# Gate and up of a SwiGLU layer in rows: both in one matmul of 512 columns, their gated product transposed on TensorE

## The chip, the cores and the metric

The kernel runs on one core of one Trainium2 chip. The metric is the device time of one execution in microseconds (us). The time of the kernel before is the median of three runs. Beside them stands one execution taken by the hardware profiler, from which the profile and the trace come.

## The reference

A hybrid decoder layer over 256 tokens of width 1024, in float32: a mixer (causal pooling and block attention) with an output projection, a cross-attention into 256 memory tokens, and a SwiGLU layer of width 2816, each with a residual and a LayerNorm behind it. The change touches the last of these:

```python
def swiglu(h, w_gate, w_up, w_down):
    return (jax.nn.silu(h @ w_gate) * (h @ w_up)) @ w_down
...
        h = layer_norm(DEEPNORM_ALPHA * h + swiglu(h, w_gate[l], w_up[l], w_down[l]),
                       ln3_g[l], ln3_b[l])
```

## The kernel before

**Three products.** Every large matmul is formed from float32 operands split in two parts, a rounded part ("h") and the rest ("l"). `three` (L217 to L221) issues three matmuls into one accumulator: h x h (L219), h x l (L220), l x h (L221). `split` (L275 to L277) makes the two parts of an activation: a cast on ScalarE (ACT) and a subtraction on VectorE (DVE).

**The weights.** `Stream` holds every weight as a list of tiles in the order of use, each 128 partitions by 1024 float32 (512 KB). For a tile, `prepare` (L68) issues the load on SyncE's queue (SP, L65, 4 raw buffers), casts it on ACT (L79) and subtracts on DVE (L80; 8 buffers for the result). `get` prepares at most one more tile at each call, up to six ahead of those that are used up (`AHEAD`), unless `held` is set; `done` counts a tile as used. The order of all instructions is the order in which the program emits them: nothing is reordered on an engine, so a cast, a Silu and a split stand in one queue on ACT, and a subtraction and a product in one on DVE. PSUM has two pools of four banks: `accbank` and `bank`.

**Before the layer.** The norm of token block 1 (128 of 256 tokens) ends while gate and up of chunk 0 are already formed for token block 0. `transpose_tok` (L283 to L289) turns the normed rows `h2` into `h2T` (channels on partitions): four transposes on TensorE (PE) into one bank (`tp`, L287), then a split.

**Gate and up.** The width of 2816 is done in 11 chunks of 256. For chunks 1 to 10 (L730 to L741) `proj_t` (L228) makes the product transposed: a 128x128 block of the weight is the stationary operand, `h2T` with its 256 tokens the moving one; for each of two halves of the chunk it walks k = 0 to 7 (8 blocks of the width 1024), first for gate (`pg`), then for up (`pu`): 2 x 2 x 8 x 3 = 96 matmuls of 256 columns. Then one Silu on ACT (L738), one product on DVE (L739), each 128x512, and one split into `gT`. Chunk 0 alone is made in rows (`first_gu`, L703): a token block of `h2T` is stationary, 256 columns of the weight move, once for gate and once for up, for token block 0 and then for token block 1. Its gated rows `sg` are transposed on PE two at a time (`first_gu_t`, L712) into `pgt`: once inside token block 1 of chunk 0, once between gate and up of chunk 1.

**Down.** `project` (L564) forms the down projection from `gT` with a token block of `gT` stationary and 512 or 256 columns of the weight moving, in five pieces of the output; four of its accumulators are `accbank` banks, the fifth is a `bank`. Behind each piece follow parts of the last norm.

Of the kernel before, what the change touches and what calls it, by code (L numbers as in the profile page):

```python
# [8 lines left out]
F32 = mybir.dt.float32  # L9
F32R = mybir.dt.float32r  # L10
AF = mybir.ActivationFunctionType
# [3 lines left out]
P = 128  # L15
D = 1024
S = 256
T = S // P
KD = D // P
CW = 256  # L20
# [4 lines left out]
NFC = DFF // CW  # L25
# [8 lines left out]
PR_BUFS = 6  # L34
# [3 lines left out]
def r32(t):  # L38
    return t.bitcast(F32)
# [63 lines left out]
@with_exitstack  # L103
def decoder_layer(
    ctx: ExitStack, tc: tile.TileContext, x, x_t, mem_t, w_in, w_u, w_pool, pool_scale, w_out,
    ln1_g, ln1_b, w_xq, w_xk, w_xkv, w_xo, ln2_g, ln2_b, w_gate, w_up, w_down, ln3_g, ln3_b, out,
):
    nc = tc.nc
    cp = ctx.enter_context(tc.tile_pool(name="const", bufs=1))
# [2 lines left out]
    sp = ctx.enter_context(tc.tile_pool(name="small", bufs=3))  # L112
# [4 lines left out]
    def a8(name, dt=F32):  # L117
        return ap.tile([P, KD, S], dt, tag="a8", name=name)

    def bank(name):  # L120
        return pb.tile([P, 512], F32, tag="b", name=name)

    def accbank(name):
        return pa.tile([P, 512], F32, tag="acc", name=name)


    ws = Stream(nc, wp)

    def cols(w, c):

        return ws.add(w[c])

    def rows(w, k0, c0, nk=2, width=D):
        return ws.add(w[k0 * P:(k0 + nk) * P, c0:c0 + width].rearrange("(k p) n -> p k n", p=P))
# [7 lines left out]
    c_xv = [rows(w_xkv, k, D) for k in range(0, KD, 2)]  # L142
    c_xq = [cols(w_xq, c) for c in range(4)]
    c_xo = [rows(w_xo, k, 0) for k in range(0, KD, 2)]
    c_gu = [(cols(w_gate, c), cols(w_up, c)) for c in range(NFC)]
    c_dn = [rows(w_down, k, 0) for k in range(0, FB, 2)]


# [34 lines left out]
    def load_gb(i, g, b):  # L183
# [15 lines left out]
    ident = cp.tile([P, P], F32, name="ident")  # L199
# [4 lines left out]
        out=tri[:, P:], in_=tri[:, P:], compare_op=OP.is_ge, fill=NEG, base=0,  # L204
# [12 lines left out]
    def three(ps, w, y, start, stop):  # L217
        (wa, wb), (ya, yb) = w, y
        nc.tensor.matmul(ps, wa, ya, start=start, stop=False)  # L219
        nc.tensor.matmul(ps, wa, yb, start=False, stop=False)  # L220
        nc.tensor.matmul(ps, wb, ya, start=False, stop=stop)  # L221

    def pair(hl, *ix):
        return hl[0][ix], hl[1][ix]

    ALL = slice(None)

    def proj_t(pss, numbers, yT, last=True):  # L228

        for f in range(2):  # L230
            for k in range(KD):
                hi, lo = ws.get(numbers, k)
                s = slice(f * P, (f + 1) * P)
                three(pss[f], (hi[:, s], lo[:, s]), pair(yT, ALL, k), k == 0, k == KD - 1)
                if f == 1 and last:
                    ws.done(numbers, k)
                yield

    def proj_n(ps, numbers, yT, t, last=True):

        for k in range(KD):
            three(ps, pair(yT, ALL, k, slice(t * P, (t + 1) * P)), ws.get(numbers, k), k == 0, k == KD - 1)
            if last:
                ws.done(numbers, k)
            yield

    def proj_rows(acc, chunks, get, pieces, first, last, free):

        last_k = sum(ws.rows(numbers) for numbers in chunks) - 1
        k0 = 0  # L250
        for numbers in chunks:
            nk = ws.rows(numbers)
            for t in sorted({piece[0] for piece in pieces}):
                for j in range(nk):
                    k = k0 + j
                    y = pair(get(k), ALL, slice(t * P, (t + 1) * P))
                    hi, lo = ws.get(numbers, j)
                    for piece in pieces:
                        if piece[0] == t:
                            s = slice(*piece[1:])  # L260
                            three(acc[piece], y, (hi[:, s], lo[:, s]), first and k == 0, last and k == last_k)
                    if free and t == pieces[-1][0]:
                        ws.done(numbers, j)
                    yield
            k0 += nk

    def run(gen, n=None):

        while n is None or n > 0:
            if next(gen, gen) is gen:  # L270
                return False
            n = None if n is None else n - 1
        return True

    def split(h, l, ps):  # L275
        nc.scalar.copy(h, ps)  # L276
        nc.vector.tensor_sub(l, ps, r32(h))  # L277
# [234 lines left out]
    class Norm:  # L512
# [11 lines left out]
        def sum(self, c0, c1, acc):  # L524
            s = slice(c0, c1)
            nc.vector.scalar_tensor_tensor(self.r[:, s], self.tok[:, s], ALPHA, acc, op0=OP.mult, op1=OP.add)  # L526
# [37 lines left out]
    def project(chunks, get, held, pieces=PIECES):  # L564

        acc = {}
        for piece in pieces:
            acc[piece] = (accbank if len(acc) < 4 else bank)("acc")[:, :piece[2] - piece[1]]
        head, rest = chunks[:-held], chunks[-held:]
        done = sum(ws.rows(numbers) for numbers in head)  # L570
        if head:
            yield from proj_rows(acc, head, get, pieces, True, False, True)
        ws.prepare(ws.used + AHEAD)
        ws.prepare(ws.used + W_BUFS, nc.gpsimd)
        ws.held = True
        for piece in pieces:
            yield from proj_rows(acc, rest, lambda k: get(done + k), [piece], not head, True, piece == pieces[-1])
            yield piece, acc[piece]

    def until(gen):  # L580

        for got in gen:
            if got is not None:
                return got
# [97 lines left out]
    h2T = (a8("h2Th", F32R), a8("h2Tl", F32R))  # L682
    gT = [(a8(f"gTh{i}", F32R), a8(f"gTl{i}", F32R)) for i in range(3)]
# [16 lines left out]
    run(xo)  # L700


    def first_gu(t):  # L703
        ps = accbank("pgn")
        for i, numbers in enumerate(c_gu[0]):
            yield from proj_n(ps[:, i * CW:(i + 1) * CW], numbers, h2T, t, t == T - 1)
        sg = sp.tile([P, 512], F32, tag="pr", name="sg", bufs=PR_BUFS)[:, :CW]
        nc.scalar.activation(sg, ps[:, :CW], AF.Silu, bias=0.0, scale=1.0)
        nc.vector.tensor_mul(sg, sg, ps[:, CW:])
        yield sg  # L710

    def first_gu_t(t, sg):  # L712
        pt = bank("pgt")
        for f in range(2):
            nc.tensor.transpose(pt[:, f * P:(f + 1) * P], sg[:, f * P:(f + 1) * P], ident)
        ts = slice(t * P, (t + 1) * P)
        split(gT[0][0][:, 0:2, ts], gT[0][1][:, 0:2, ts], pt[:, :CW].rearrange("p (f t) -> p f t", f=2))

    gu0 = first_gu(0)
    run(gu0, 14)  # L720
    transpose_tok(h2T, h2[:, 1, :], 1, 0)
    run(gu0, 2)
    gu1 = first_gu(1)
    transpose_tok(h2T, h2[:, 1, :], 1, 4)
    sg0 = until(gu0)
    ws.held = False
    run(gu1, 6)
    first_gu_t(0, sg0)
    sg1 = until(gu1)
    for c in range(1, NFC):  # L730
        pg = accbank("pg").rearrange("p (f t) -> p f t", f=2)
        pu = bank("pu").rearrange("p (f t) -> p f t", f=2)
        run(proj_t([pg[:, f, :] for f in range(2)], c_gu[c][0], h2T))
        if c == 1:
            first_gu_t(1, sg1)
        run(proj_t([pu[:, f, :] for f in range(2)], c_gu[c][1], h2T))
        sg = sp.tile([P, 2, S], F32, name="sgt", tag="pr", bufs=PR_BUFS)
        nc.scalar.activation(sg, pg, AF.Silu, bias=0.0, scale=1.0)  # L738
        nc.vector.tensor_mul(sg, sg, pu)  # L739
        i, f = divmod(2 * c, KD)  # L740
        split(gT[i][0][:, f:f + 2, :], gT[i][1][:, f:f + 2, :], sg)  # L741


    def store(t, y, c0, c1):
# [1 line left out]

    pieces = PIECES[:3] + ((1, 512, 768), (1, 768, D))
    dn = project(c_dn, lambda k: (gT[k // KD][0][:, k % KD], gT[k // KD][1][:, k % KD]), 3, pieces)
    for t in range(T):
        norm = Norm(3, h2[:, t, :])  # L750
        for _, c0, c1 in [piece for piece in pieces if piece[0] == t]:
            acc = until(dn)[1]
            for c in range(0, c1 - c0, 256):
                norm.add(c0 + c, c0 + c + 256, acc[:, c:c + 256])
        norm.stats()
        aside = (D - 384, D)
        norm.centre(*aside)
        norm.centre(0, 512)
        norm.scale_aside(*aside)
        norm.scale(0, 512)  # L760
        store(t, norm.r, 0, 512)
        norm.centre(512, aside[0])
        norm.scale(512, aside[0])
        store(t, norm.r, 512, D)
# [1 line left out]


_INS = ["x", "x_t", "mem_t", "w_in", "w_u", "w_pool", "pool_scale", "w_out", "ln1_g", "ln1_b", "w_xq", "w_xk",
        "w_xkv", "w_xo", "ln2_g", "ln2_b", "w_gate", "w_up", "w_down", "ln3_g", "ln3_b"]


# [30 lines left out]
```

## Time and profile before

| what | value |
|---|---|
| median of 3 runs | 394.28 us (394.07 to 394.31) |
| the profiled execution's own time | 393.67 us |
| its span, first to last instruction | 391.6 us |
| instructions | 6504 |
| granted clock of TensorE | 0.996 |
| HBM read, over the span | 70.52 MB, 183 GB/s read and written |

How to read the profile: engines are PE (TensorE matmul), PEld (TensorE loading a stationary operand, which overlaps PE), DVE, ACT, POOL (GpSimd) and SP or SPq (the queue that issues loads). In a row of the timeline the first number is the start in us from the start of the span, the second the length in us; then engine, line of the kernel, operation, what it writes and reads, its shape, and in brackets idle time ahead of it with what ended that. Matmuls are pipelined and their ends are modelled, so one lists longer than the distance to the next; the distance from start to start is what a stream of them costs. In a row of a group, behind the bar stand busy us in total and mean ns of one, then idle us ahead of the group and what released it.

### The profile page before, as it was taken

The numbers are of one execution on the slowest core, as the hardware profiler recorded it, in microseconds if no ns is written. First come the engines' busy times: TensorE is split into PE (matmuls) and PEld (weight loads), VectorE is DVE, ScalarE is ACT, GpSimd is POOL, SyncE is SP. The second block draws the span as 40 slices with busy tenths as digits, with TensorE's granted clock in tenths as the row PEclk, the third lists the DMA queues.
The fourth block names the chain that finished last, engine by engine and source line by source line (L and its number), as shares of the span: only waits on it lengthen the run. The fifth ranks groups of instructions, "written<-read, shape, count | busy, mean of one in ns | idle before, by whom it ended". The sixth has DMA issues, their size and how long they took to land.

```text
span 391.6 us, 6504 instructions
## 1 busy us (share of the span) xinstructions
PE 381.3 (97%) x2651; PEld 353.6 (90%) x2651; DVE 244.6 (62%) x327; ACT 176.1 (45%) x253; POOL 31.0 (8%) x37
## 2 busy tenths in 40 slices
PE   8999999999999999999999999999999999999991
PEld 7997889898888899988899999999999998888881
DVE  2749998776388766656887744556644457543276
ACT  3745848455233645455245633355543335343000
POOL 1000006500420000001400000000000000000022
PEclk9999999999999999999999999999999999999998
DMA  7998544756606862234408756654445875753002
GB/s 239 336 329 273 200 166 148 273 174 228 236 9 220 281 251 109 110 107 161 162 3 279 241 177 216 216 179 173 144 170 197 277 258 163 256 175 108 1 27 82
DMA packets 21886, 71.99 MB, mean 184 GB/s; under 512 B 2784, under 2 KB 3552, under 8 KB 21728
## 3 DMA queue, kind: packets, MB, share of 16 engines
q1 hardware_dynamic: 21568, 71.05, 52.7%
q10 hardware_dynamic: 288, 0.52, 0.7%
q8 instruction: 21, 0.34, 0.3%
q14 instruction: 9, 0.07, 0.1%
HBM read 70.52 MB, written 1.05 MB: 183 GB/s over the span
## 4 chain that ended last, share of the span: by engine, by line
PE 95%; DMA 2%; DVE 1%; SPq 0%; ACT 0%; issue 0%; DVEq 0%
PE acc L220 9%; PE acc L219 9%; PE acc L221 9%; PE pu L219 6%; PE pu L220 6%; PE pu L221 6%; PE pqk L323 5%; PE pg L220 5%; PE pg L219 5%; PE pg L221 5%; PE pxk L219 2%; PE pxq L219 2%; PE pxq L221 2%; PE pxq L220 2%; PE pxk L220 2%; PE pxk L221 2%
## 5 line engine op out<-in xcount | busy, mean ns | idle before, releaser
L739 DVE TENSOR_TENSOR sgt<-sgt,pu 128x512 f32<-128x512 f32 x10 | 6.9, 688 | 42.4 <-PE pu L221 42.4
L276 ACT CAST gTh<-sgt 128x512 fp32r<-128x512 f32 x10 | 6.2, 620 | 56.5 <-DVE sgt L739 56.5
L537 POOL TENSOR_TENSOR rs<-rs,mhalf 128x1 f32<-128x1 f32 x6 | 5.5, 912 | 199.0 <-DVE rs L536 199.0
L526 DVE SCALAR_TENSOR_TENSOR r<-h,acc 128x256 f32<-128x256 f32 (+1 forms) x12 | 6.0, 502 | 11.5 <-PE acc L221 11.5
L356 ACT ACTIVATE pr<-pr,mx 128x128 f32<-128x128 f32 (+1 forms) x16 | 7.2, 449 | 11.0 <-DVE mx L367 10.7
L547 ACT ACTIVATE r<-r,rs 128x384 f32<-128x384 f32 x2 | 1.2, 616 | 22.8 <-POOL rs L537 22.8
L277 DVE TENSOR_TENSOR gTl<-sgt,gTh 128x512 fp32r<-128x512 f32 x10 | 6.9, 693 | 6.9 <-ACT gTh L276 6.9
L541 DVE SCALAR_TENSOR_TENSOR r<-r,mv,g 128x512 f32<-128x512 f32 (+2 forms) x14 | 10.7, 776 | 0.0
L356 ACT ACTIVATE xpr<-xs,mx 128x256 f32<-128x256 f32 x8 | 3.7, 469 | 12.4 <-DVE mx L367 12.4
L529 DVE BATCH_NORM_STATS2 st<-r 128x6 f32<-128x512 f32 (+1 forms) x16 | 9.0, 561 | 0.5
L429 POOL TENSOR_TENSOR win<-upad 128x271 f32<-128x271 f32 x4 | 3.6, 888 | 59.9 <-DVE pr L363 59.9
L80 POOL TENSOR_TENSOR w59l<-w59r,w59h 128x1024 fp32r<-128x1024 f32 x1 | 2.4, 2442 | 69.9 <-ACT w59h L79 69.9
L276 ACT CAST h2Th<-tp 128x512 fp32r<-128x512 f32 x4 | 2.3, 587 | 12.3 <-PE tp L287 12.3
L738 ACT ACTIVATE sgt<-pg 128x512 f32<-128x512 f32 x10 | 6.0, 596 | 3.6 <-PE pg L221 3.6
L552 DVE SCALAR_TENSOR_TENSOR h<-r,rs,b 128x512 f32<-128x512 f32 x8 | 6.0, 752 | 1.9 <-POOL rs L537 1.8
L277 DVE TENSOR_TENSOR xTl<-xr,xTh 128x512 fp32r<-128x512 f32 (+1 forms) x5 | 2.9, 580 | 6.2 <-ACT xTh L276 6.2
L429 POOL TENSOR_TENSOR win<-win 128x269 f32<-128x269 f32 (+2 forms) x6 | 6.7, 1118 | 0.5
L526 DVE SCALAR_TENSOR_TENSOR r<-xt,acc 128x512 f32<-128x512 f32 x4 | 2.7, 682 | 6.2 <-PE acc L221 6.2
L361 DVE RECIPROCAL sm<-sm 128x2 f32<-128x2 f32 x12 | 2.0, 165 | 5.9 <-ACT xpr L356 4.5
L367 DVE TENSOR_REDUCE mx<-xs 128x2 f32<-128x512 f32 x4 | 2.8, 691 | 4.4 <-PE xs L221 4.4
L79 ACT CAST w41h<-w41r 128x1024 fp32r<-128x1024 f32 x1 | 1.1, 1051 | 9.5 <-PE tp L287 9.5
L287 PE MATMUL tp<-ident,h 128*128 128x128 f32 x32 | 4.8, 274 | 0.1
(1075 smaller groups left out, 1661.8 us busy)
## 6 DMA issues: line engine op xcount, KB each, us to landing
g<-in_ln_g SPq DMA_DIRECT2D x3, 512.0 KB, 6.3
b<-in_ln_b SPq DMA_DIRECT2D x3, 512.0 KB, 6.9
mr<-in_mem_t SPq DMA_DIRECT2D x1, 1024.0 KB, 7.9
xt<-in_x SPq DMA_DIRECT2D x1, 1024.0 KB, 9.0
out<-r SPq DMA_DIRECT2D x4, 256.0 KB, 2.0
xr<-in_x_t SPq DMA_DIRECT2D x3, 256.0 KB, 6.3
w2r<-in_w_in SPq DMA_DIRECT2D x1, 512.0 KB, 7.0
w3r<-in_w_in SPq DMA_DIRECT2D x1, 512.0 KB, 7.8
```

Source lines behind the costliest of these rows:

```text
L219: nc.tensor.matmul(ps, wa, ya, start=start, stop=False)
L220: nc.tensor.matmul(ps, wa, yb, start=False, stop=False)
L221: nc.tensor.matmul(ps, wb, ya, start=False, stop=stop)
L276: nc.scalar.copy(h, ps)
L277: nc.vector.tensor_sub(l, ps, r32(h))
L323: nc.tensor.matmul(qk[i][:, f, :], w, y, start=k == 0 and f == 0 and n == 0, stop=k == KD - 1 and n == 2, skip_group_check=True)
L356: nc.scalar.activation(dst[:, j, :], src[:, j, :], AF.Exp, bias=mx[:, j:j + 1], scale=1.0, accum_out=sm[:, j:j + 1])
L429: nc.gpsimd.tensor_add(nxt[:, 2 * n - 1:], cur[:, 2 * n - 1:], cur[:, n - 1:PADW + S - n])
L526: nc.vector.scalar_tensor_tensor(self.r[:, s], self.tok[:, s], ALPHA, acc, op0=OP.mult, op1=OP.add)
L529: nc.vector.bn_stats(self.st[:, self.n, :], self.r[:, c0:c1])
L541: nc.vector.scalar_tensor_tensor(self.r[:, s], self.r[:, s], self.mv[:, 0:1], gb[self.i][0][:, s], op0=OP.subtract, op1=OP.mult)
L739: nc.vector.tensor_mul(sg, sg, pu)
```

## The change

All 11 chunks are formed in rows. Host code puts gate's and up's 256 columns of a chunk side by side in one array (`w_gu`), so that a weight tile holds two k of 512 columns where it held four of 256. `proj_n` takes several accumulators: for each k it issues three matmuls of 512 columns for token block 0 and three for token block 1, each block with its own `accbank`. Chunk 0 runs token block 0 first (7 steps, a `transpose_tok`, the last step, the second `transpose_tok`), then token block 1. `gated` makes Silu and product of one token block (128x256 each). `gated_t` transposes the gated rows of a chunk, four transposes into one bank, and splits them into `gT`; for chunk c - 1 it is issued three k steps into chunk c, for the last chunk four steps into the down projection.

```diff
-    c_gu = [(cols(w_gate, c), cols(w_up, c)) for c in range(NFC)]
+    c_gu = [ws.add(w_gu[c], 4) for c in range(NFC)]
...
-    def proj_n(ps, numbers, yT, t, last=True):
+    def proj_n(pss, numbers, yT, last=True):
         for k in range(KD):
-            three(ps, pair(yT, ALL, k, slice(t * P, (t + 1) * P)), ws.get(numbers, k), k == 0, k == KD - 1)
+            for t, ps in pss.items():
+                three(ps, pair(yT, ALL, k, slice(t * P, (t + 1) * P)), ws.get(numbers, k), k == 0, k == KD - 1)
             if last:
                 ws.done(numbers, k)
             yield
...
+    def gated(c, t, ps):
+        sg = sgs[c][:, t, :]
         nc.scalar.activation(sg, ps[:, :CW], AF.Silu, bias=0.0, scale=1.0)
         nc.vector.tensor_mul(sg, sg, ps[:, CW:])
...
+    def gated_t(c):
+        pt = bank("pgt").rearrange("p (f t) -> p f t", f=2)
+        for t in range(T):
+            for f in range(2):
+                nc.tensor.transpose(pt[:, f, t * P:(t + 1) * P], sgs[c][:, t, f * P:(f + 1) * P], ident)
+        i, f = divmod(2 * c, KD)
+        split(gT[i][0][:, f:f + 2, :], gT[i][1][:, f:f + 2, :], pt)
+
+    sgs = [sp.tile([P, T, CW], F32, name="sg", tag="pr", bufs=PR_BUFS)]
+    first = [accbank("pg") for t in range(T)]
+    gu0 = proj_n({0: first[0]}, c_gu[0], h2T, False)
+    run(gu0, 7)
     transpose_tok(h2T, h2[:, 1, :], 1, 0)
+    run(gu0)
+    gated(0, 0, first[0])
     transpose_tok(h2T, h2[:, 1, :], 1, 4)
     ws.held = False
+    run(proj_n({1: first[1]}, c_gu[0], h2T))
+    gated(0, 1, first[1])
     for c in range(1, NFC):
+        sgs.append(sp.tile([P, T, CW], F32, name="sg", tag="pr", bufs=PR_BUFS))
+        pss = {t: accbank("pg") for t in range(T)}
+        gu = proj_n(pss, c_gu[c], h2T)
+        run(gu, 3)
+        gated_t(c - 1)
+        run(gu)
+        for t in range(T):
+            gated(c, t, pss[t])
...
     dn = project(c_dn, lambda k: (gT[k // KD][0][:, k % KD], gT[k // KD][1][:, k % KD]), 3, pieces)
+    run(dn, 4)
+    gated_t(NFC - 1)
...
+    given["w_gu"] = np.concatenate([chunks(given["w_gate"]), chunks(given["w_up"])], axis=3)
```

More of the change, by code (lines that the diff above doesn't have):

```diff
@@ L105, in decoder_layer @@
     ctx: ExitStack, tc: tile.TileContext, x, x_t, mem_t, w_in, w_u, w_pool, pool_scale, w_out,
-    ln1_g, ln1_b, w_xq, w_xk, w_xkv, w_xo, ln2_g, ln2_b, w_gate, w_up, w_down, ln3_g, ln3_b, out,
+    ln1_g, ln1_b, w_xq, w_xk, w_xkv, w_xo, ln2_g, ln2_b, w_gu, w_down, ln3_g, ln3_b, out,
 ):
@@ L700, in decoder_layer @@
     run(xo)
[L703 to L707, printed above, removed]
+    def gated(c, t, ps):
+        sg = sgs[c][:, t, :]
         nc.scalar.activation(sg, ps[:, :CW], AF.Silu, bias=0.0, scale=1.0)
         nc.vector.tensor_mul(sg, sg, ps[:, CW:])
[L710 to L717, printed above, removed]
@@ L719, in decoder_layer @@
-    gu0 = first_gu(0)
-    run(gu0, 14)
+    def gated_t(c):
[7 more added lines that the diff above has]
+    first = [accbank("pg") for t in range(T)]
@@ L721, in decoder_layer @@
+    gu0 = proj_n({0: first[0]}, c_gu[0], h2T, False)
+    run(gu0, 7)
     transpose_tok(h2T, h2[:, 1, :], 1, 0)
-    run(gu0, 2)
-    gu1 = first_gu(1)
+    run(gu0)
+    gated(0, 0, first[0])
     transpose_tok(h2T, h2[:, 1, :], 1, 4)
-    sg0 = until(gu0)
     ws.held = False
-    run(gu1, 6)
-    first_gu_t(0, sg0)
-    sg1 = until(gu1)
+    run(proj_n({1: first[1]}, c_gu[0], h2T))
+    gated(0, 1, first[1])
     for c in range(1, NFC):
[L731 to L741, printed above, removed]
+        sgs.append(sp.tile([P, T, CW], F32, name="sg", tag="pr", bufs=PR_BUFS))
[6 more added lines that the diff above has]
+            gated(c, t, pss[t])
@@ L768 @@
 _INS = ["x", "x_t", "mem_t", "w_in", "w_u", "w_pool", "pool_scale", "w_out", "ln1_g", "ln1_b", "w_xq", "w_xk",
-        "w_xkv", "w_xo", "ln2_g", "ln2_b", "w_gate", "w_up", "w_down", "ln3_g", "ln3_b"]
+        "w_xkv", "w_xo", "ln2_g", "ln2_b", "w_gu", "w_down", "ln3_g", "ln3_b"]
 def kernel(**inputs):
@@ L790 @@
     given["w_u"], given["w_xk"] = chunks(given["w_in"][:, :512]), chunks(given["w_xkv"][:, :D])
-    for name in ("w_xq", "w_gate", "w_up"):
-        given[name] = chunks(given[name])
+    given["w_xq"] = chunks(given["w_xq"])
+    given["w_gu"] = np.concatenate([chunks(given["w_gate"]), chunks(given["w_up"])], axis=3)
     for name in _INS:
```

## The prediction

> **What bounds the kernel now.** I read the page first: busy shares, granted clock, the chain that ended last. Times are microseconds (us).
>
> ```profile
> PE 381.3 (97%) x2651; PEld 353.6 (90%) x2651; DVE 244.6 (62%) x327; ACT 176.1 (45%) x253; POOL 31.0 (8%) x37
> ...
> PEclk9999999999999999999999999999999999999998
> ...
> PE 95%; DMA 2%; DVE 1%; SPq 0%; ACT 0%; issue 0%; DVEq 0%
> ```
>
> TensorE (PE) is busy 97% of the span, its clock is granted in full, and 95% of the chain is PE. A busy PE proves little, since its ends are modelled; so the second view is who waited for whom, for PE alone.
>
> ```profile
> PE busy L299 <- POOL ident masks.py:199: 1.4, 1, 1.4
> PE pqk L323 <- DVE w2l L80: 0.6, 1, 0.6
> PE pqk L323 <- ACT w0h L79: 0.3, 1, 0.3
> ```
>
> That is all: PE waits 2.3 us, at the start. From then on the time is the sum of PE's spacings, start to start. In the gate and up stage a spacing taken away is a saving, and one added is a loss, one for one. Third view: two stretches side by side, one of 512-column matmuls, one of the gate and up stage (256 columns). The columns are length, then busy time and count of PE, PEld, DVE, ACT and POOL, then granted clock, DMA share and GB/s.
>
> ```profile
> 91.00:111.00 20.00, 20.00 (x90) 16.57 (x89) 11.85 (x16) 7.90 (x9) 5.75 (x3) 1.00 0.55 190
> 207.50:322.00 114.50, 114.50 (x956) 114.50 (x956) 61.63 (x62) 52.04 (x62) 0.00 (x0) 1.00 0.61 209
> ```
>
> With 256 columns the loading of stationary operands (PEld) never rests; with 512 it rests a sixth of the time. DVE and ACT are about half idle in the stage.
>
> **The change part by part.** *Fewer, longer matmuls.* One chunk is now 96 matmuls of 256 columns (gate and up, 2 halves, 8 k, 3 products). After, it is 48 of 512 columns (8 k, 2 token blocks, 3 products), with the activations stationary and the weights moving. The down projection already runs that form. The timeline of PE gives both spacings.
>
> ```profile
> 311.08 0.28 PE L219 MATMUL pg<-h2Th,w97h 128*128 128x256 f32 x1
> ...
> 322.60 0.40 PE L219 MATMUL acc<-w101h,gTh 128*128 128x512 f32 x1
> ```
> ```profile
> 371.08 0.39 PE L219 MATMUL acc<-w117h,gTh 128*128 128x512 f32 x1
> ...
> 375.16 0.39 PE L219 MATMUL acc<-w117h,gTh 128*128 128x512 f32 x1
> ```
>
> Chunk 10 lies between the first two rows: 96 matmuls in 11.52 us, 0.1200 each. Between the last two lie 6 weight tiles of 3 products: 18 matmuls in 4.08 us, 0.2267 each. Two of the short cost 0.2400, one of the long 0.2267: each pair replaced saves 13.3 ns. A chunk's matmuls shrink from 11.52 to 48 x 0.2267 = 10.88, by 0.64; over 11 chunks (528 pairs) that is 7.0 us.
>
> *Forty more transposes.* Before, only chunk 0 transposes (4 instructions, two pairs). After, every chunk has a block of 4: 44 in all. What a block costs among 512-column matmuls is read from blocks of the same shape elsewhere.
>
> ```profile
> 122.02 0.60 PE L287 MATMUL tp<-ident,h 128*128 128x128 f32 x4
> 122.37 0.48 PE L219 MATMUL xv<-w37h,mTh 128*128 128x512 f32 x1
> 122.69 0.39 PE L220 MATMUL xv<-w37l,mTh 128*128 128x512 f32 x1
> ...
> 125.23 0.60 PE L287 MATMUL tp<-ident,h 128*128 128x128 f32 x4
> ```
> ```profile
> 166.05 0.60 PE L639 MATMUL xpt<-ident,xpr 128*128 128x128 f32 x4
> ...
> 170.62 0.28 PE L219 MATMUL xs<-xkTh,xq 128*128 128x256 f32 x1
> ```
>
> In the first rows it is 3.21 us from block to block, of which 12 matmuls (2 k, 2 pieces, 3 products) are 2.72: 0.49 for the block. In the second pair the block has 18 matmuls behind it: 4.57 - 4.08 = 0.49 again. Of this 0.44 are the transposes and the long gap behind the first matmul (122.02 to 122.69, less 0.227); the other 0.05 are the next gaps, which read 0.23 to 0.24. The second case has 18 matmuls against 12 and costs no more, so the slower gaps end.
>
> The profile lists one transpose at 274 ns:
>
> ```profile
> L287 PE MATMUL tp<-ident,h 128*128 128x128 f32 x32 | 4.8, 274 | 0.1
> ```
>
> That is one's time from start to end; four overlap, and the next matmul starts 0.35 after the first (122.02 to 122.37). The Trainium skill, "TensorE: Matmul & The Clock Gate", Part 4: PE-mode transpose, gives about 275 ns for one in a kernel: this agrees as a duration. Laid end to end, a block by that page would be 1.10 us, and the change would lose (a rival, below).
>
> *Chunk 0.* It is held by the norm, so its first half gains nothing.
>
> ```profile
> 199.87 0.75 DVE L552 SCALAR_TENSOR_TENSOR h<-r,rs,b 128x512 f32<-128x512 f32 x1
> ...
> 200.77 0.63 PE L287 MATMUL tp<-ident,h 128*128 128x128 f32 x4
> ```
>
> The second block of h2 transposes for token block 1 starts 0.15 after DVE has made that half of h2 (199.87 + 0.75 = 200.62). The norm's work on DVE is not moved, and PE comes there no later after the change; so 200.77 stays, and I count from there. The Silu and product of token block 0 now stand ahead of the second block's split on ACT and DVE (0.4 us each). That split feeds k = 4, which in the new order comes 12 long matmuls (2.7 us) after the block: covered. Without the cover it would cost 0.4, once.
>
> *The sum.* Before, from 200.77 to the down projection at 322.60: 121.83. After: the h2 block 0.49, token block 1 of chunk 0 24 x 0.2267 = 5.44, ten chunks of 10.88 + 0.49 = 113.70; together 119.63. That is 2.20 less. The block of chunk 10 lies behind the first four steps of the down projection: +0.49, less some 0.04, because those steps no longer begin behind 256-column matmuls, where the same slow gaps stood. Sum: **-1.75 us**.
>
> *What ACT and DVE do.* Per chunk, ACT's Silu becomes two of 256 columns, DVE's product two; the split reads PSUM instead of SBUF.
>
> ```profile
> L739 DVE TENSOR_TENSOR sgt<-sgt,pu 128x512 f32<-128x512 f32 x10 | 6.9, 688 | 42.4 <-PE pu L221 42.4
> ...
> L738 ACT ACTIVATE sgt<-pg 128x512 f32<-128x512 f32 x10 | 6.0, 596 | 3.6 <-PE pg L221 3.6
> ```
> ```profile
> 208.43 1.05 ACT L79 CAST w65h<-w65r 128x1024 fp32r<-128x1024 f32 x1 [2.07 <-DMA w65r<-in_w_gate]
> 209.38 0.38 ACT L708 ACTIVATE sg<-pgn 128x256 f32<-128x256 f32 x1
> ```
> ```profile
> 209.51 1.23 DVE L80 TENSOR_TENSOR w65l<-w65r,w65h 128x1024 fp32r<-128x1024 f32 x1 [1.27 <-ACT w65h L79]
> 210.65 0.41 DVE L709 TENSOR_TENSOR sg<-sg,pgn 128x256 f32<-128x256 f32 x1
> ```
>
> ACT goes from 0.60 to 0.77 per chunk, DVE from 0.69 to 0.82: hidden, both are half idle. But here the change adds its one new **wait**: PE's transposes need the product, and behind them in PE's queue stand the rest of the chunk's matmuls. Their cover is the three k steps ahead of them, 18 x 0.2267 = 4.08 us. The product needs, from the chunk's last matmul, about 0.2 for its end, 0.38 and 0.41: some 1.1 to 1.3. So 2.8 us are to spare. In chunk 0 less: as the rows show, Silu stands behind the cast of w65, which waited for its load, and the product ended at 211.06. That load is issued when w61's slot is free, and the Silu and product of token block 0 no longer stand between the h2 split and w61's cast: some 0.3 earlier, so the product ends near 210.75. PE wants it for the third transpose: chunk 1 starts at 200.77 + 0.49 + 5.44 = 206.70, and 206.70 + 4.08 + 0.22 is 211.0. I put 0 to 0.3 on this and take 0.1.
>
> *Loads.* The same bytes in the same 512 KB tiles and 4 KB runs; a tile lasts 2.84 us instead of 2.88. Nothing is moved on SP's queue but by these amounts, and POOL does nothing in the stage. In the down projection accumulators 2 and 3 take the banks of chunk 10; they are wanted 2.7 us into it, the products are read out by 1.0.
>
> The sum is made on the profiled execution (span 391.6, its own time 393.67): 393.67 - 1.65 = 392.0. The runs' median, 394.28, lies 0.61 above it; with the same difference I predict **392.6 us**.
>
> **The rivals.** *A wait takes the place of the gain (slower).* Place: ACT's strict queue in each chunk, where the Silu of a chunk stands behind the fourth weight cast, and that behind a load. Point: it decides once the product comes more than 2.8 us late, and from 0.17 us of waiting per chunk (1.65 in 10) nothing is left. Rows for the loads' time to landing:
>
> ```profile
> w101r<-in_w_down SPq DMA_DIRECT2D x1, 512.0 KB, 5.5
> ...
> w105r<-in_w_down SPq DMA_DIRECT2D x1, 512.0 KB, 9.1
> ```
> ```profile
> ACT gTh L276 <- DVE sgt L739: 50.8, 9, 6.0
> ```
>
> For it: ACT has waited for loads, 2.07 before w65's cast. If a third of that, 0.7, came on top of the cover in every chunk, the time would be 392.6 + 7.0 = 399.6. Against it: ACT spent 50.8 us idle before the split's cast, work done and waiting for the product; the fourth load of a chunk is issued when DVE is through with the fourth tile of the chunk before. That is some 8.7 us into it by my count (split's cast at 4.6, two casts of 1.05 and two subtractions of 1.23 behind it, partly side by side), so even 9.1 us to landing ends 8.7 + 9.1 - 11.4 = 6.4 us into its own chunk, and its cast and subtraction end by 9. Chance 0.09.
>
> *PE prices the instructions otherwise (slower).* If transposes filled PE for their listed 274 ns, 11 blocks cost 0.61 more each: 392.6 + 6.7 = 399.3. If a 512-column matmul saved less against two short ones, each 1 ns less would be 0.53 us. From the rows, 226.7 - 120.0 = 106.7 ns is what 256 more columns cost, and 13.3 ns is left as the fixed part of either: halving the count saves that part. The Trainium skill, "TensorE: Matmul & The Clock Gate", section "Back-to-back issue gap", has N/2.4 + 2.5 ns for a full clock: its slope agrees with these rows, its 2.5 ns does not. By that page 528 pairs would save 1.3 us instead of 7.0, and the kernel would take 398.3. Both are against rows of the same shapes; chance 0.04.
>
> *The stage is fed, not computed (no change).* If PE were paced by weight tiles, shorter matmuls would only wait: about 394.3. Against it: no wait of PE in the stage, and tiles are prepared up to six ahead. Chance 0.06.
>
> *More than that (faster).* If the blocks cost only their 0.44 and the gaps behind them vanished, 0.55 less, and another 0.5 from steps I hold for covered or fixed (the norm): 391.5. Chance 0.03.
>
> **How the numbers follow.** The forecast has 0.78, with its own range: block 0.44 to 0.51, chunk 0 0 to 0.3, and 0.3 each way for the 0.6 between profiled execution and median: 391.7 to 393.4. To hold 8 in 10 I take in part of the fed case: 391.5 to 393.8. A measurement of this kernel can tell about 0.2% (0.8 us) from no change, so faster is under 393.5: 0.78 and 0.03 make 0.81. Within 0.2%: the fed case and a small wait, 0.07. Slower: 0.12.
>
> **What would show it.** Right: rows of 128x512 in the stage 0.227 apart; blocks pgt x4 between them costing 0.49; no wait of PE on the product; the down projection starting near 320.4 instead of 322.60; 528 matmuls fewer and 40 transposes more. Wrong: PE waiting for the product in the list of waits (first rival); gaps of 0.232 or more throughout a chunk (second); PE waiting on weight tiles (third).

## The result, and the profile after

The changed kernel takes 392.45 us (median; three executions from 391.81 to 392.49), the kernel before 394.29: a ratio of 0.9953 (95% interval 0.9938 to 0.9969). One further execution, the profiled one, ran nearly throughout at a granted clock of 0.56 (634.47 us), as did one of a later experiment, with one step of cover, at 0.66 (542.63 us); why stays open, and neither counts here. The trace read here is therefore that of the same kernel run again: 392.1 us, span 390.1, ratio 0.9947 (0.9930 to 0.9964). The gain is half a per cent, small but clear of the noise in both measurements.

Busy shares, granted clock and chain of the changed kernel's page:

```profile
PE 378.6 (97%) x2163; PEld 329.2 (84%) x2163; DVE 246.8 (63%) x336; ACT 176.5 (45%) x262; POOL 31.0 (8%) x37
...
PEclk9999999999999999999999999999999999999997
...
PE 83%; DVE 6%; DMA 4%; ACT 3%; POOL 1%; issue 1%; SPq 0%; ACTq 0%; POOLq 0%; DVEq 0%
```

PE has 488 instructions fewer (2651 before), which is 528 matmuls less and 40 transposes more, at the same busy share; PEld fell from 90% to 84%. The chain holds less PE than before, though PE is no less the bound. The list of waits of PE says why:

```profile
PE busy L300 <- POOL ident masks.py:199: 1.4, 1, 1.4
PE pqk L324 <- ACT w0h L79: 0.9, 1, 0.9
PE pqk L324 <- DVE w2l L80: 0.8, 1, 0.8
PE tp L288 <- DVE h L553: 0.3, 1, 0.3
```

The waits for weight tiles (`pqk`) are at the start of the program, as before. The last row is new: PE now comes 0.3 us too early to the transposes of `h2`, and from there the chain is followed back through the norm. None of PE's waits is for the gated product. The two stretches of windows (length; busy time and count of PE, PEld, DVE, ACT, POOL; clock; DMA share; GB/s) show the stage's matmuls behaving as the 512-column stretch did before:

```profile
91.00:111.00 20.00, 20.00 (x90) 16.57 (x89) 11.71 (x16) 7.90 (x9) 5.76 (x3) 1.00 0.57 196
207.50:319.00 111.50, 111.50 (x512) 92.24 (x511) 63.63 (x71) 52.11 (x70) 0.00 (x0) 1.00 0.64 211
```

PEld is busy 83% of either. The timeline of PE: the second block of h2 transposes, two of the new blocks with the first matmul of chunk 2 between them, and the start of the down projection:

```profile
201.00 0.63 PE L288 MATMUL tp<-ident,h 128*128 128x128 f32 x4
...
211.03 0.60 PE L714 MATMUL pgt<-ident,sg 128*128 128x128 f32 x4
...
218.31 0.39 PE L219 MATMUL pg<-w65h,h2Th 128*128 128x512 f32 x1
...
222.39 0.60 PE L714 MATMUL pgt<-ident,sg 128*128 128x128 f32 x4
...
320.61 0.39 PE L219 MATMUL acc<-w101h,gTh 128*128 128x512 f32 x1
```

From the second h2 block to the down projection it is 119.61 us (before: 322.60 - 200.77 = 121.83); from block to block 11.36. Between 218.31 and 222.39 lie 18 matmuls of 512 columns: 0.2267 each, as the same shape took in the down projection before.

### The profile page after: what moved, and what is told of

Its sections match the earlier page's. It is cut to its first block, busy times and chain, and to the rows that moved or that the text cites. A ratio compares the mean times of both kernels' runs of the same rounds, so it can differ in the third digit from the quotient of the medians.

```text
span 632.4 us, 5533 instructions
## 1 busy us (share of the span) xinstructions
PE 622.0 (98%) x2163; PEld 433.3 (69%) x2163; DVE 249.4 (39%) x336; ACT 177.8 (28%) x262; POOL 28.9 (5%) x37
## 4 chain that ended last, share of the span: by engine, by line
PE 97%; DMA 1%; DVE 1%; SPq 0%; ACT 0%; issue 0%; DVEq 0%
PE pg L219 11%; PE pg L220 11%; PE pg L221 11%; PE acc L220 9%; PE acc L221 9%; PE acc L219 9%; PE pqk L324 5%; PE pxk L219 2%; PE pxq L219 2%; PE xv L219 2%; PE pxk L221 2%; PE xv L220 2%; PE xv L221 2%; PE pxq L221 2%; PE pxq L220 2%; PE pxk L220 2%
## 5 line engine op out<-in xcount | busy, mean ns | idle before, releaser
L708 DVE TENSOR_TENSOR sg<-sg,pg 128x256 f32<-128x256 f32 x22 | 9.3, 421 | 77.2 <-ACT sg L707 77.2
L707 ACT ACTIVATE sg<-pg 128x256 f32<-128x256 f32 x22 | 8.5, 385 | 89.0 <-PE pg L221 89.0
L278 DVE TENSOR_TENSOR gTl<-pgt,gTh 128x512 fp32r<-128x512 f32 x11 | 7.6, 692 | 52.8 <-ACT gTh L277 52.8
L277 ACT CAST gTh<-pgt 128x512 fp32r<-128x512 f32 x11 | 6.5, 587 | 61.9 <-PE pgt L714 61.9
L357 ACT ACTIVATE pr<-pr,mx 128x128 f32<-128x128 f32 (+1 forms) x16 | 7.2, 448 | 13.3 <-DVE mx L368 13.1
L714 PE MATMUL pgt<-ident,sg 128*128 128x128 f32 x44 | 10.5, 390 | 0.0
L714 PEld LDWEIGHTS pgt<-ident,sg 128*128 128x128 f32 x44 | 7.5, 179 | 4.3 <-issue 3.1
L278 DVE TENSOR_TENSOR h1Tl<-tp,h1Th 128x512 fp32r<-128x512 f32 x4 | 2.8, 692 | 16.9 <-ACT h1Th L277 16.9
L288 PEld LDWEIGHTS tp<-ident,h 128*128 128x128 f32 x32 | 5.4, 179 | 3.5 <-issue 2.8
L277 ACT CAST h1Th<-tp 128x512 fp32r<-128x512 f32 x4 | 2.4, 588 | 19.5 <-PE tp L288 19.5
L288 PE MATMUL tp<-ident,h 128*128 128x128 f32 x32 | 7.6, 397 | 0.0
```

Source lines behind the costliest of these rows:

```text
L288: nc.tensor.transpose(ps[:, k * P:(k + 1) * P], tok[:, (k0 + k) * P:(k0 + k + 1) * P], ident)
L357: nc.scalar.activation(dst[:, j, :], src[:, j, :], AF.Exp, bias=mx[:, j:j + 1], scale=1.0, accum_out=sm[:, j:j + 1])
L714: nc.tensor.transpose(pt[:, f, t * P:(t + 1) * P], sgs[c][:, t, f * P:(f + 1) * P], ident)
```

## The experiments

All run on one core, in three groups, each beside the kernel before (393.9, 394.3 and 393.7); ratios are to that kernel in the same group. The changed kernel, 392.1, ran in the first group only, with the first four experiments. The executions of one kernel in one group differ by up to 3 us, part of it ahead of the stage (which began between 193.70 and 195.44), so the length of the stage (first gate matmul to first matmul of the down projection) is compared as well; before it is 128.63 (193.97, the row below, to 322.60, a row that the prediction shows).

```profile
193.97 0.37 PE L219 MATMUL pgn<-w57h,h2Th 128*128 128x256 f32 x1
```

**The changed kernel again, for its trace.**

> The changed kernel once more, unaltered, for its trace at a full clock. The theory (13.3 ns saved per pair of 256-column matmuls, 0.49 us paid per block of four transposes, nothing waited for): 392.4 us; 128x512 matmuls of the stage 0.227 us apart, chunk to chunk 11.37 us, the down projection starting at 320.4 in the trace instead of 322.60. Rival, the same net from other terms: a chunk of about the same 11.37 but with blocks clearly under 0.45 and matmuls clearly over 0.228 apart, or with waits of PE on the product.

Measured: 392.1, the stage 126.41 (194.20 to 320.61), and the rows above. The theory's numbers stand, and none of the rival's signs is there; the start of the down projection, 320.61, is 0.2 later than named only because the whole stage began 0.23 later.

**Without the transposes.** `gated_t` splits the gated rows as they are.

```diff
-        pt = bank("pgt").rearrange("p (f t) -> p f t", f=2)
-        for t in range(T):
-            for f in range(2):
-                nc.tensor.transpose(pt[:, f, t * P:(t + 1) * P], sgs[c][:, t, f * P:(f + 1) * P], ident)
...
-        split(gT[i][0][:, f:f + 2, :], gT[i][1][:, f:f + 2, :], pt)
+        split(gT[i][0][:, f:f + 2, :], gT[i][1][:, f:f + 2, :], sgs[c])
```

> The changed kernel without the transposes: the gated rows are split as they are, so the part of the computation that turns them is left out, with all of PE's blocks pgt; the rest stays. The theory: 11 blocks at 0.49 us, less 0.04: 5.35 us off the changed kernel's 392.4, that is 387.0. Rival, blocks that cost only 0.3 (and a smaller gain from the longer matmuls): 389.1. Rival, transposes that fill PE for their listed 274 ns (11 x 1.10): 380.3.

Measured: 387.13. The timeline of PE in that kernel:

```profile
194.20 0.48 PE L219 MATMUL pg<-w57h,h2Th 128*128 128x512 f32 x1
...
315.74 0.39 PE L219 MATMUL acc<-w101h,gTh 128*128 128x512 f32 x1
```

The stage is 121.54: 4.87 less for the ten blocks within it, 0.487 each. The block of 0.49 is shown, and with it what the longer matmuls alone would bring: 1.8% (ratio 0.9825, 0.9803 to 0.9847). The transposes hand three quarters of that back.

**Rows, but 256 columns.** Each 512-column matmul becomes two.

```diff
-                three(ps, pair(yT, ALL, k, slice(t * P, (t + 1) * P)), ws.get(numbers, k), k == 0, k == KD - 1)
+                y, (hi, lo) = pair(yT, ALL, k, slice(t * P, (t + 1) * P)), ws.get(numbers, k)
+                for i in range(2):
+                    s = slice(i * CW, (i + 1) * CW)
+                    (ya, yb) = y
+                    for n, (st, mv) in enumerate(((ya, hi), (ya, lo), (yb, hi))):
+                        nc.tensor.matmul(ps[:, s], st, mv[:, s], start=k == 0 and i == 0 and n == 0,
+                                         stop=k == KD - 1 and n == 2, skip_group_check=True)
```

> The changed kernel with each 512-column matmul made as two of 256 columns, first gate's then up's, into the two halves of the same bank: rows and transposes stay, only the count and the width of the matmuls go back. The theory: 13.3 ns for each of the 504 pairs behind the norm of the second token block (the 24 pairs ahead of it are hidden by that wait), 6.7 us, less about 0.05 per block since a block among 256-column matmuls has no slow gaps behind it (0.5): 398.6. Rival, a fixed part of only 2.5 ns per matmul: 1.3 us more than the changed kernel, 393.7.

Measured: 398.81, slower than before (1.0115, 1.0095 to 1.0135). The timeline:

```profile
194.55 0.37 PE L248 MATMUL pg<-w57h,h2Th 128*128 128x256 f32 x1
...
327.09 0.40 PE L219 MATMUL acc<-w101h,gTh 128*128 128x512 f32 x1
```

The stage is 132.54, 6.13 more than in the changed kernel; with the 0.05 per block that falls away (0.5, the prediction's figure) it is 6.6, or 13.2 ns for each of 504 pairs. Rows and transposes alone cost; the whole gain is the width. The Trainium skill ("TensorE: Matmul & The Clock Gate", "Back-to-back issue gap") gives its N/2.4 + 2.5 ns for a single matmul on its own, and says that in a stream the loads count too. Taken for the pace of this stream all the same, its 2.5 ns would have given 393.7 (an estimate); these runs decide for 13.3.

**The transposes twice.** The loop over a block's four transposes runs two times.

> The changed kernel with each block's four transposes issued twice in a row, into the same places. The theory: what a block costs is nearly all in the transposes themselves, about 0.0875 to 0.11 us each by the start of the next matmul; 44 more of them 3.9 to 4.8 us: 396.3 to 397.2. Rival, the block's 0.49 is mostly the switch between transposes and matmuls, which stays one per block: under 394.5. Rival, 274 ns each: 404.5.

Measured: 396.79. The timeline shows eight in a row, and the stage:

```profile
194.09 0.48 PE L219 MATMUL pg<-w57h,h2Th 128*128 128x512 f32 x1
...
305.14 1.03 PE L714 MATMUL pgt<-ident,sg 128*128 128x128 f32 x8
...
324.60 0.39 PE L219 MATMUL acc<-w101h,gTh 128*128 128x512 f32 x1
```

The stage is 130.51, 4.10 more for the 40 added transposes within it: 0.1025 each, though each is listed at about 271 ns (the row is that of the changed kernel; with the transposes twice it has 88 at 272):

```profile
L714 PE MATMUL pgt<-ident,sg 128*128 128x128 f32 x44 | 6.6, 271 | 0.0
```

So 0.41 of a block's 0.487 are its four transposes; the other 0.08 go to the slow gaps behind. That transposes fill PE for their duration is refuted.

**One step of cover.** `run(gu, 3)` ahead of `gated_t` becomes `run(gu, 1)`. The cover is the work that PE has ahead of the transposes while the product is made.

> The changed kernel with the transposes of a chunk one k step into the next instead of three: the cover of the product shrinks from 4.08 to 1.36 us. The theory (the product is there 1.04 us behind the chunk's last matmul, as 219.35 against 218.31 in the changed kernel's trace): nine of the ten blocks wait for nothing; only chunk 0's, whose product ended at 210.73 behind the cast of w65, makes PE wait, from about 208.5 on: 2.3 us, once. 394.4. Rival, the three steps are needed in every chunk since ACT and DVE are behind with weights: over 400.

> The kernel with one step of cover once more, for its trace at a full clock. The theory: one wait of PE for the product, 1.8 to 2.3 us in chunk 0's block, none in the other nine, whose blocks then follow 11.37 apart; where the time is near 396 instead of 394, the granted clock drops behind that one wait for some 3 us. Rival: waits in several blocks.

Measured: ratio 1.0025 (1.0005 to 1.0046), in two groups: four executions from 393.9 to 394.4, as expected, and five from 395.8 to 397.5. The mean granted clock of an execution divides them alike: 0.993 to 0.994 in the four, 0.989 to 0.992 in the five. The trace (395.46, clock 0.988) is of the second kind. Its timeline of PE and its windows:

```profile
207.81 0.38 PE L714 MATMUL pgt<-ident,sg 128*128 128x128 f32 x2
210.31 0.69 PE L714 MATMUL pgt<-ident,sg 128*128 128x128 f32 x2 [2.12 <-DVE sg L708]
223.04 0.60 PE L714 MATMUL pgt<-ident,sg 128*128 128x128 f32 x4
234.40 0.60 PE L714 MATMUL pgt<-ident,sg 128*128 128x128 f32 x4
```
```profile
208.00:210.00 2.00, 0.19 (x2) 0.00 (x0) 1.30 (x2) 0.95 (x2) 0.00 (x0) 1.00 0.83 256
210.00:212.00 2.00, 1.69 (x5) 1.48 (x6) 0.99 (x2) 1.81 (x3) 0.00 (x0) 0.57 0.98 360
212.00:214.00 2.00, 2.00 (x7) 1.53 (x6) 2.00 (x3) 1.71 (x2) 0.00 (x0) 0.58 0.89 272
214.00:216.00 2.00, 2.00 (x10) 1.67 (x9) 1.92 (x3) 1.06 (x1) 0.00 (x0) 1.00 0.83 252
```

There is one wait, in chunk 0's block; the others are 11.36 apart, so one step covers them. Behind the wait the granted clock (the third number from the end) is 0.57 and 0.58 for 4 us, which loses (0.43 + 0.42) x 2 = 1.7 us. So this single wait of 2.1 us costs twice: itself, and in five of nine executions some 1.7 to 2 more through the clock.

**No cover.** `gated_t(c - 1)` stands directly ahead of the chunk.

> The changed kernel with the transposes of a chunk directly ahead of the next chunk's matmuls: no cover. The theory: each of nine blocks waits for the product, 1.04 us behind the chunk's last matmul plus about 0.1, of which some 0.2 are used by the first two transposes: 0.9 each, 8.3 in all; chunk 0's block waits from 206.94 to 210.73, 3.8; together 12: 404. Rival, PE has other work to fill with or the product comes sooner: under 398.

Measured: 406.39 (1.0303, 1.0280 to 1.0327). PE's list of waits begins:

```profile
PE pgt L714 <- DVE sg L708: 7.5, 19, 3.1
```
```profile
223.31 0.44 PE L714 MATMUL pgt<-ident,sg 128*128 128x128 f32 x2 [0.25 <-DVE sg L708]
223.99 0.44 PE L714 MATMUL pgt<-ident,sg 128*128 128x128 f32 x2 [0.24 <-DVE sg L708]
...
235.60 0.44 PE L714 MATMUL pgt<-ident,sg 128*128 128x128 f32 x2 [0.25 <-DVE sg L708]
```
```profile
211.00:213.00 2.00, 2.00 (x7) 1.58 (x7) 1.57 (x2) 1.96 (x3) 0.00 (x0) 0.63 1.00 395
213.00:215.00 2.00, 2.00 (x6) 1.52 (x6) 2.00 (x3) 1.50 (x3) 0.00 (x0) 0.51 0.56 141
...
223.00:320.00 97.00, 93.06 (x412) 73.66 (x412) 49.17 (x56) 40.83 (x55) 0.00 (x0) 1.00 0.50 169
```

From chunk to chunk it is 12.29 in the timeline (223.31 to 235.60): 0.92 more than 11.37, as expected. Each block waits twice, once for each token block's product; the list shows only 0.49 of the 0.92, because it counts idle time from the modelled ends of the matmuls. The stage is 139.63 long, 13.22 more than in the changed kernel: 9 x 0.92 = 8.3, about 3.2 at chunk 0's block (listed as 3.06), and what is over, 1.7, is again the clock, 0.63 and 0.51 in the windows from 211 to 215. Behind the short waits, from 223 on, the clock stays at 1.00. This is the first rival's mechanism with its price: it is real, and the steps ahead of the transposes keep it away, one of them in nine blocks, the three of the changed kernel in chunk 0's.

**Two chunks' transposes together.** In every second chunk `gated_t(c - 2)` and `gated_t(c - 1)`.

> The changed kernel with the transposes of two chunks together: eight in a row in every second chunk, four behind the first steps of the down projection as now. The theory (a block's cost is nearly linear in its transposes: eight in a row cost 0.90 in the kernel with doubled transposes, four 0.485): five blocks fewer save 0.07 each, 0.3 us: 391.8. Rival, a fixed price per switch of 0.15 or more: 0.75 us or more, under 391.4.

Measured: 392.18 (0.9945, 0.9927 to 0.9964): by time no different from the changed kernel. The stage is 126.06 (194.59 to 320.65), 0.35 shorter: 0.07 for each of five blocks saved. That is the theory's size, read from one trace of each; it is too small for the times to tell.

**PE's waits at the norm filled.** Beside the pairing (`early_1` issues four matmuls of chunk 1: token block 0, k 0 and 1, rounded weights):

```diff
-    gu0 = proj_n({0: first[0]}, c_gu[0], h2T, False)
-    run(gu0, 7)
...
+    ws.prepare(len(ws.tiles) + 1, nc.gpsimd)
+    run(proj_n({0: first[0]}, c_gu[0], h2T, False))
     transpose_tok(h2T, h2[:, 1, :], 1, 0)
-    run(gu0)
+    early_1()
     gated(0, 0, first[0])
```

> The paired kernel, and beside that PE's waits at the norm of the second token block filled: chunk 0's eight steps for token block 0 run through, then the first block of h2 transposes, then four matmuls of chunk 1 (token block 0, k 0 and 1, the two products with the rounded weights), whose tile is prepared early, its subtraction on POOL. The theory: PE loses 0.46 and 0.29 us there in the changed kernel's trace, and both are filled: 0.7 us less than paired, 391.1. Rival, the norm or the weight tile comes later in turn (POOL has the norm's power in its queue, DVE and ACT the splits): no gain over paired, 391.8 or more.

Measured: 393.77 (0.9985, 0.9972 to 0.9999), slower than paired: the theory failed. As the rival said, the norm came later, but not for the reasons that it gave (the queues). DVE's and POOL's timelines in that kernel:

```profile
199.26 2.85 DVE L553 SCALAR_TENSOR_TENSOR h<-r,rs,b 128x512 f32<-128x512 f32 x1 [0.44 <-POOL rs L538]
```
```profile
199.19 2.37 POOL L80 TENSOR_TENSOR w61l<-w61r,w61h 128x1024 fp32r<-128x1024 f32 x1
```

The norm's step, 0.75 in the seven others of this shape, took 2.85: it ended 0.55 behind POOL's subtraction, which had begun just ahead of it, and PE waited 1.74 for it. To test that, POOL was left out (the edit is against the kernel just above):

```diff
-    ws.prepare(len(ws.tiles) + 1, nc.gpsimd)
...
+    ws.fetch(i + 1, nc.sync)
...
+    nc.scalar.copy(hi_1, ws.raws[i])
...
     transpose_tok(h2T, h2[:, 1, :], 1, 4)
+    nc.vector.tensor_sub(lo_1, ws.raws[i], r32(hi_1))
```

> The filled kernel with POOL left alone: the early weight tile is only cast on ACT ahead of the norm's end, and its subtraction follows on DVE behind the second h2 split. The theory (in the filled kernel the norm's step on DVE took 2.85 us instead of 0.75, just while POOL subtracted, and that alone undid the gain): the step takes 0.75 again, PE's waits of 0.46 and 0.29 at the norm are filled, 0.7 us less than the paired kernel's 392.2: 391.5, and the down projection starts some 0.7 earlier behind the first matmul of the stage. Rival, the filling itself delays the norm or its splits: 392.2 or more, with the step at 0.75.

Measured: 391.14 (0.9931, 0.9906 to 0.9955), the fastest median of the kernels that compute the whole layer. DVE's and PE's timelines:

```profile
199.88 0.75 DVE L553 SCALAR_TENSOR_TENSOR h<-r,rs,b 128x512 f32<-128x512 f32 x1 [0.44 <-POOL rs L538]
```
```profile
195.44 0.48 PE L219 MATMUL pg<-w57h,h2Th 128*128 128x512 f32 x1
...
320.71 0.39 PE L219 MATMUL acc<-w101h,gTh 128*128 128x512 f32 x1
```

The step is back at 0.75, and the stage 125.27: 0.79 less than paired, 1.14 less than the changed kernel. It beats the kernel before; that it beats the changed one rests on the stage's length, since the intervals of the times overlap. The filled kernel's waits are gone too: in its list of waits PE waits for `h` no more.

**Rows of 128 columns**, as in the kernel with 256, but four to a bank.

> The changed kernel with each 512-column matmul made as four of 128 columns into the quarters of the same bank. If each matmul costs 13.3 ns beside its columns, whatever their number, a short one takes 66.7 ns and the kernel (504 places behind the norm) 392.3 + 20 = 412. Rival, the loading of the stationary operand sets a floor: two loads of about 0.19 us that overlap, 0.0875 (the transposes' spacing) to 0.096 apart: 392.3 + 62 to 79 = 454 to 471.

Measured: 506.93, beyond both. Loads and matmuls are 0.1117 apart (36 in 4.02 us), though each load is listed at 0.19; two rows of PEld:

```profile
249.88 0.19 PEld L248 LDWEIGHTS pg<-w66l,h2Th 128*128 128x128 f32 x1
249.99 0.19 PEld L248 LDWEIGHTS pg<-w66h,h2Tl 128*128 128x128 f32 x1
```

There is a floor, as the rival said, but it lies higher than the transposes' spacing had led to expect: (4 x 0.1117 - 0.2267) x 528 is 116, against 115 measured. That it is the load which sets this floor is not shown: every matmul here has its own load, so a limit of the loads and another limit per matmul look alike. At 256 columns a matmul takes 0.120, just above it.

## Why the prediction was right

- **Bound and sum.** "So 200.77 stays, and I count from there": the count from that block to the down projection was 119.63, and the trace has 119.61. The block itself came at 201.00, since the whole stage began 0.23 later for reasons ahead of it; from the first gate matmul to it, the distance is 6.80 in both traces. The block in the down projection was put at +0.45; from its first matmul to the end of the span it is 69.49 against 69.00. With the 0.23 the span fell by 1.5 and not by 1.75.
- **The last step to the forecast was partly luck.** The sum gave 392.0 for a profiled execution, and 0.6 was added because the median before lay that much above its profile. In the run again the profiled execution (392.09) and the median (392.1) are alike. So the trace bears out the 392.0; that the forecast of 392.6 lies so near the first median of 392.45 owes something to chance.
- **13.3 ns per pair.** This saving is shown by the rows of 256 columns (13.2). The rival with 2.5 ns fell. What the 13.3 consists of stays open: the prediction calls it a fixed part of each matmul, but only two widths went into that, and at 256 columns the loads never rest.
- **0.49 per block.** This is shown by leaving the blocks out (0.487). The rival with 274 ns each fell with the doubled transposes (0.1025).
- **The norm holds chunk 0.** This is shown: PE waits there for `h`, and filling the place shortened the stage.
- **The cover.** The product was put 1.1 to 1.3 behind the chunk's last matmul. DVE's timeline in the changed kernel has the products of chunk 0 and of chunk 1:

```profile
210.32 0.41 DVE L708 TENSOR_TENSOR sg<-sg,pg 128x256 f32<-128x256 f32 x1
...
218.93 0.42 DVE L708 TENSOR_TENSOR sg<-sg,pg 128x256 f32<-128x256 f32 x1 [0.26 <-ACT sg L707]
```

The second ends at 219.35, and chunk 2 begins at 218.31: 1.04. One step of cover is enough for nine blocks. Chunk 0's needs more: its product ended at 210.73 and PE wanted it at 211.25. No wait came, so the 0.1 taken for it was not spent. That the product ended so near the forecast 210.75 is in part chance, since the stage had begun 0.23 later; counted from the h2 block, the product came a quarter of a microsecond sooner than forecast, and the margin was twice what was forecast.

- **What the price of a wait left out.** The first rival prices a wait as its own length. For short waits in every chunk, which it had in mind, this holds: without cover they cost 0.92 a chunk at a clock of 1.00. For one long wait it does not: 2.1 or 3.1 us of idle PE at chunk 0's block brought up to 1.7 more through the clock, which the prediction has nowhere.
- **Fed, not computed.** This rival fell: without the transposes the same loads fed a stage 4.9 shorter, and PE waited for no weight tile in it.

## What to carry to other kernels

Price a PE instruction by the distance from its start to the next, never by its listed duration, and price an added kind of instruction by rows of the same shape in the same surroundings. The net here is the small difference of 7 us gained and 5 lost, and a coarse price for either would have had the wrong sign. Half as many matmuls for the same columns saved 13.3 ns for each one less; transposes that this needs cost their spacing, so the trade pays where the transposed result is small against the matmuls. An added wait of PE has to be covered where its producer is at its latest (here the first chunk, behind a weight load), not where it usually is, and one long wait can cost more than its length.

## What the runs showed of the hardware

- In these kernels a matmul of 512 columns takes 226.7 ns from start to start and one of 256 takes 120.0: 106.7 ns per 256 columns and 13.3 ns beside. One of 128 columns takes 111.7, where this line would give 66.7; each has its own load of the stationary operand, and which of the two sets that floor is not separated.
- PE idle for 2.1 us (208.19 to 210.31) was followed by a granted clock of 0.57 over some 4 us, in the trace and, by the mean clocks, in five of nine other executions. Waits of 0.92 in every chunk, and one of 1.74 in the filled kernel, left the clock at 1.00 in their traces. The Trainium skill, "TensorE: Matmul & The Clock Gate", Part 1, has the clock halve after an idle window of about 3.4 us: here a shorter wait did it, though not each time.
- A DVE operation with two inputs in SBUF took 2.85 us instead of 0.75 beside a POOL operation that began just ahead of it; without POOL the delay was gone. The Trainium skill, "SBUF — State Buffer", section "SBUF: two separate sides", describes the ports that the two share as an exclusive lock held for a whole instruction. These rows agree but for a remainder: a step blocked to POOL's end would end 0.75 behind it, and this one ended 0.55 behind it (spans on POOL are rough).
